# Row norms taken out of the first transposes and applied to the projections' results

## The chip, the cores and the metric

One core of a Trainium2 chip runs the whole program: one launch, all inputs in the chip's memory, float32 throughout. The metric is the device time of one execution in microseconds (us), as a median of several runs. The engines are named as in the profile: PE is TensorE (matmuls), PEld its weight loads, DVE is VectorE, ACT is ScalarE, POOL is GpSimd, SP is the engine whose queue issues most of the transfers.

## What is computed

A transformer block with a mixture of experts, followed by a convolution and recurrence block, for 256 tokens of 1024 numbers. The change touches only the beginning of the first block:

```python
hn = rmsnorm(h, attn_norm_g[layer])          # h is x, 256 x 1024
proj = hn @ w_in[layer]                      # 1024 x 2560
q, k, v, u, vg = jnp.split(proj, [512, 1024, 1536, 2048], axis=-1)
sb_out = stick_breaking_attention(q, k, v)
sg_out = chunked_spatial_gating(u, vg, ...)  # gelu(u) * mix(rmsnorm(gelu(vg)))
...
def rmsnorm(x, g):
    return x * lax.rsqrt(jnp.mean(x * x, axis=-1, keepdims=True) + EPS) * g
```

The root mean square of a row of x is one factor per token. It can be multiplied into the rows before the matmul or into the rows of the result.

## The kernel before

The kernel keeps x as the tile `h` (128 partitions, two chunks c of 128 tokens, 1024 columns). A matmul contracts over partitions, so x is transposed first: 8 column blocks kt of 128 times 2 chunks, into four PSUM tiles `pts` (two named `acc`, two named `zt`). Every weight and activation of the projections is split into a rounded part (`hi`, type fp32r) and the remainder (`lo`), and each product is three matmuls: hi·hi, lo·hi, hi·lo.

Lines 285 to 289 make the row factors: for each chunk ACT squares 1024 columns with a running sum (`ssq`), DVE turns the sum to a mean plus epsilon (`ms`, line 252), POOL raises it to -0.5 (`r1`, line 253), and DVE writes `diag`, the identity times the 128 factors. The transposes at line 300 are matmuls of `h` against `diag`, so that the rows come out transposed and scaled at once. Lines 301 to 308 split the transposed blocks: ACT writes `xT_hi` with the column gains `gcol` as its scale, DVE writes `xT_lo`. `gcol` itself is a transpose of the loaded gain rows (line 291) that DVE copies out.

The weights arrive as tiles of 1 MB in a ring of buffers, issued by SP in order; a buffer is issued again when its reader has freed it. A weight tile of the first projections is handled in four parts, called units. `Units.split` (lines 213 to 234) has ACT copy a unit to `w_hi` (line 228) and DVE, or POOL for units 30 to 39, subtract to get `w_lo` (line 229). There are three buffers of each, so the `w_hi` of unit u+3 waits until PE has finished unit u. `proj_ws(j)` (line 314) does one projection of 256 columns with the weights as the stationary side, so that the tokens lie along the free side of the result; `proj_ts(j)` (line 328) has the tokens on the partitions. Projections 0 to 3 give q and k (copied to SBUF by ACT, lines 350 and 352), 4 and 5 give v (copied by DVE, lines 446 and 450), 6 and 7 give vg, 8 and 9 give u. `gelu2` (line 428) computes gelu from a projection's PSUM tile in five steps that go back and forth between ACT and DVE; the mixing (line 488) needs the u tile `uT`, and the projection's PSUM buffer is free only after gelu2's last step (line 436).

The order of the instructions on each engine is set when the program is built, by a list scheduler with times of its own; on the chip each engine then runs its queue in that order. Before the first data has landed PE runs 12 matmuls on constants (`keep_warm`, line 186).

Of the kernel before, what the change touches and what calls it, by code (L numbers as in the profile page):

```python
# [8 lines left out]
F32 = mybir.dt.float32  # L9
# [3 lines left out]
AF = mybir.ActivationFunctionType  # L13
OP = mybir.AluOpType
# [78 lines left out]
def kernel(ctx: ExitStack, tc: tile.TileContext, a: dict, out):  # L93
    nc = tc.nc
    V, S, T, G = nc.vector, nc.scalar, nc.tensor, nc.gpsimd
# [57 lines left out]
    p1 = phase.enter_context(tc.tile_pool(name="p1", bufs=1, side="right"))  # L153
# [4 lines left out]
    p1m = work.enter_context(tc.tile_pool(name="p1m", bufs=1, side="right"))  # L158
    p1t = work.enter_context(tc.tile_pool(name="p1t", bufs=3, side="right"))
    attn = ExitStack()  # L160
    p1w = attn.enter_context(tc.tile_pool(name="p1w", bufs=2))
    psA = phase.enter_context(tc.tile_pool(name="psA", bufs=3, space=PSUM))
    psZ = phase.enter_context(tc.tile_pool(name="psZ", bufs=2, space=PSUM))
    h = keep.tile([128, 2, 1024], F32, name="h")
# [10 lines left out]
    ident = consts.tile([128, 128], F32, name="ident")  # L175
# [73 lines left out]
    def rms_scale(dst, ssq, n, mul=1.0):  # L249

        t = small.tile([128, ssq.shape[1]], F32, name="ms")
        V.tensor_scalar(t, ssq, mul / n, mul * EPS, op0=OP.mult, op1=OP.add)
        G.tensor_tensor(dst, t, mhalf[:, :ssq.shape[1]], op=OP.pow)
# [27 lines left out]
    hnl = [(p1, R)[i].tile([128, 4, 256], F32R, name=f"xT_lo{i}", tag=("a1", "r2")[i]) for i in range(2)]  # L281
    ssq = small.tile([128, 2, 2], F32, name="ssq")
    r1 = small.tile([128, 2], F32, name="r1")
    diag = p1.tile([128, 2, 128], F32, name="diag", tag="x40")
    for c in range(2):
        sq = psZ.tile([128, 1024], F32, name="zt")
        S.activation(sq, h[:, c], AF.Square, accum_out=ssq[:, c, 0:1])
        rms_scale(r1[:, c:c + 1], ssq[:, c, 0:1], 1024)
        V.tensor_scalar(diag[:, c], ident, r1[:, c:c + 1], None, op0=OP.mult)
    pg = psA.tile([128, 24], F32, name="acc")  # L290
    T.transpose(pg, rows, ident[:24, :24])
    V.tensor_copy(gcol, pg)
# [1 line left out]
    gffn = gcol[:, 16:24]  # L294
    V.tensor_mul(wr, wr, gffn[:, :, None].to_broadcast([128, 8, 40]))
    units.prep(0)
    pts = [(psA, psA, psZ, psZ)[kk].tile([128, 2, 2, 128], F32, name=("acc", "acc", "zt", "zt")[kk]) for kk in range(4)]
    for kt in range(8):
        for c in range(2):
            T.matmul(pts[kt // 2][:, kt % 2, c], h[:, c, kt * 128:(kt + 1) * 128], diag[:, c], start=True, stop=True)  # L300
    for kk in range(4):
        for kt in (2 * kk, 2 * kk + 1):
            S.activation(hnh[kt // 4][:, kt % 4], pts[kt // 2][:, kt % 2].rearrange("p c t -> p (c t)"), AF.Copy,
                         scale=gcol[:, kt:kt + 1])
        for kt in (2 * kk, 2 * kk + 1):
            V.scalar_tensor_tensor(hnl[kt // 4][:, kt % 4], pts[kt // 2][:, kt % 2].rearrange("p c t -> p (c t)"),
                                   gcol[:, kt:kt + 1], hnh[kt // 4][:, kt % 4].bitcast(F32), op0=OP.mult,
                                   op1=OP.subtract)
        if kk < 2:
            units.prep(kk + 1)  # L310

    XT = [[x[k // 4][:, k % 4] for k in range(8)] for x in (hnh, hnl)]

    def proj_ws(j):

        ps = psA.tile([128, 2, 256], F32, name="acc")
        for part in range(4):
            wh, wl = units.get(U_IN[j] + part)
            for b in range(2):
                for k in range(2):  # L320
                    kt = 2 * part + k
                    for i, (w, x) in enumerate(((wh, XT[0]), (wl, XT[0]), (wh, XT[1]))):
                        T.matmul(ps[:, b, :], w[:, k, b * 128:(b + 1) * 128], x[kt],
                                 start=kt == 0 and b == 0 and i == 0, stop=kt == 7 and i == 2, skip_group_check=True)
            units.prep(U_IN[j] + part + 3)
        return ps

    def proj_ts(j):

        ps = psA.tile([128, 2, 256], F32, name="acc")  # L330
        for part in range(4):
            wh, wl = units.get(U_IN[j] + part)
            for c in range(2):
                for k in range(2):
                    kt = 2 * part + k
                    for i, (w, x) in enumerate(((wh, XT[0]), (wl, XT[0]), (wh, XT[1]))):
                        T.matmul(ps[:, c, :], x[kt][:, c * 128:(c + 1) * 128], w[:, k, :],
                                 start=kt == 0 and c == 0 and i == 0, stop=kt == 7 and i == 2, skip_group_check=True)
            units.prep(U_IN[j] + part + 3)
        return ps  # L340

    qT = R.tile([128, 4, 256], F32, name="qT", tag="r3")
    kT = R.tile([128, 4, 256], F32, name="kT", tag="r4")
    vt = p1.tile([128, 2, 512], F32, name="vt", tag="x40")
    vg2 = p1m.tile([128, 2, 512], F32, name="vg2", tag="x41")
    mixh = [p1d.tile([128, 4, 256], F32R, name="mix_hi")]
    mixl = [p1d.tile([128, 4, 256], F32R, name="mix_lo")]

    for j in range(2):
        S.activation(qT[:, 2 * j:2 * j + 2], proj_ws(j), AF.Copy)  # L350
    for j in range(2):
        S.activation(kT[:, 2 * j:2 * j + 2], proj_ws(2 + j), AF.Copy)

# [72 lines left out]
    def gelu2(dst, ps):  # L428

        s = p1t.tile([128, 512], F32, name="gel", tag="tmp")  # L430
        f = ps.rearrange("p b t -> p (b t)")
        S.activation(s, f, AF.Square)
        V.tensor_scalar(s, s, GELU_A, 1.0, op0=OP.mult, op1=OP.add)
        V.tensor_mul(s, s, f)
        S.activation(s, s, AF.Tanh, scale=GELU_C)
        V.scalar_tensor_tensor(dst, s.rearrange("p (b t) -> p b t", b=2), 1.0, ps, op0=OP.add, op1=OP.mult)
# [6 lines left out]
                    channel_multiplier=1)  # L443

    ps = proj_ts(4)
    V.tensor_copy(vt[:, :, 0:256], ps)
    probs(0)
    scores(2)
    ps = proj_ts(5)
    V.tensor_copy(vt[:, :, 256:512], ps)  # L450
    heads_out(0)
    probs(1)
    scores(3)
    ps = proj_ts(6)
    gelu2(vg2[:, :, 0:256], ps)
    heads_out(1)
    probs(2)
    ps = proj_ts(7)
    gelu2(vg2[:, :, 256:512], ps)
    heads_out(2)  # L460
    probs(3)
# [10 lines left out]
    for c in range(2):  # L472
        sq = p1t.tile([128, 512], F32, name="gel", tag="tmp")
# [2 lines left out]
    G.tensor_tensor(rv, ssv, mhalf[:, :2], op=OP.pow)  # L476
    for c in range(2):
        V.scalar_tensor_tensor(vg2[:, c], vg2[:, c], rv[:, c:c + 1], gb512, op0=OP.mult, op1=OP.mult)
    ps = proj_ws(8)
    gelu2(uT[:, 0:2], ps)  # L480
    heads_out(3)
    attn.close()
    ring.open("c", late.enter_context(tc.tile_pool(name="ring_c", bufs=NC, reuse_waits="tile")), NC)
    ring.pump()
    ps = proj_ws(9)
    gelu2(uT[:, 2:4], ps)

    def mixing(p):
# [81 lines left out]
    for j in range(4):  # L570
        acc = psA.tile([128, 2, 256], F32, name="acc")
# [11 lines left out]
    for j in range(4):  # L583
        acc = psA.tile([128, 2, 256], F32, name="acc")
# [64 lines left out]
    pr = psM.tile([128, 2, 32], F32, name="ms")  # L649
# [135 lines left out]
    start = gather(0, 1)  # L785
# [148 lines left out]
    r1 = small.tile([128, 2], F32, name="r1")  # L934
# [27 lines left out]
    for i in range(16):  # L962
# [37 lines left out]
        for k, idx in enumerate(W_EXP[i]["w_down"]):  # L1000
            t = ring.get(idx)
            for n in range(2):
                for j in range(2):
                    m = T.matmul(dn[n][64 * j:64 * j + 64], hT[:, k, 64 * j:64 * j + 64], t[:, j, 512 * n:512 * n + 512],  # L1004
                             start=k == 0, stop=k == 3, skip_group_check=True)
# [16 lines left out]
    for n in range(2):  # L1022
        for k, idx in enumerate(W_EXP[15]["w_down"]):
# [3 lines left out]
            for j in range(2):  # L1027
                T.matmul(dn[n][64 * j:64 * j + 64], hT[:, k, 64 * j:64 * j + 64], t[:, j, 512 * n:512 * n + 512],
                         start=k == 0, stop=k == 3, skip_group_check=True)
# [21 lines left out]
    diag = q0.tile([128, 2, 128], F32, name="diag2")  # L1051
# [506 lines left out]
```

## Time and profile before

| | |
|---|---|
| median of 3 runs | 1062.04 us |
| lowest and highest run | 1059.91 and 1063.41 us |
| the profiled execution's own time | 1064.05 us |
| span of its records | 1062.3 us |
| PE busy in the span | 1030.8 us (97%) |
| DVE, ACT, POOL busy | 531.5, 368.4, 226.6 us |
| moved by DMA | 300.23 MB |

The profiled execution is 2.0 us above the median of the runs, and 1.7 us of its time lies outside the span of the records. The stages follow each other: transposes and first projections to about 88 us, output projection and routing to 123 us, the experts to 582 us, the second block to the end.

A row of the timeline gives start, duration, engine, line, operation, written tile and read tiles, shapes and count, and in brackets the idle time of the engine before it with what ended it. Several equal instructions in a row are merged into one line of the timeline, whose duration goes from the first start to the last end.

### The profile page before, as it was taken

The numbers are of one execution on the slowest core, as the hardware profiler recorded it, in microseconds if no ns is written. First come the engines' busy times: TensorE is split into PE (matmuls) and PEld (weight loads), VectorE is DVE, ScalarE is ACT, GpSimd is POOL, SyncE is SP. The second block draws the span as 40 slices with busy tenths as digits, with TensorE's granted clock in tenths as the row PEclk, the third lists the DMA queues.
The fourth block names the chain that finished last, engine by engine and source line by source line (L and its number), as shares of the span: only waits on it lengthen the run. The fifth ranks groups of instructions, "written<-read, shape, count | busy, mean of one in ns | idle before, by whom it ended". The sixth has DMA issues, their size and how long they took to land.

```text
span 1062.3 us, 16320 instructions
## 1 busy us (share of the span) xinstructions
PE 1030.8 (97%) x6660; PEld 742.5 (70%) x6660; DVE 531.5 (50%) x1014; ACT 368.4 (35%) x595; POOL 226.6 (21%) x135
## 2 busy tenths in 40 slices
PE   8999999999999999999999999996999999999997
PEld 7998644444444444444443999876999999998996
DVE  4758432222222222222223588888947676556555
ACT  5565311000000000000001654857546446444443
POOL 0262000000000000000000887654876900000000
PEclk9999999999999999999999999998999999999999
DMA  9987899899999999999999855422553666655531
GB/s 317 303 349 275 313 366 411 332 409 409 409 409 409 409 409 409 409 408 409 409 408 387 259 192 178 141 80 80 199 164 118 202 211 198 199 189 177 192 116 40
DMA packets 139131, 300.23 MB, mean 283 GB/s; under 512 B 14341, under 2 KB 79341, under 8 KB 139053
## 3 DMA queue, kind: packets, MB, share of 16 engines
q1 hardware_dynamic: 138541, 297.84, 76.3%
q8 instruction: 53, 0.87, 0.3%
q10 hardware_dynamic: 432, 1.05, 0.3%
q0 software_dynamic: 80, 0.26, 0.1%
q14 instruction: 25, 0.20, 0.1%
HBM read 298.08 MB, written 1.05 MB: 282 GB/s over the span
## 4 chain that ended last, share of the span: by engine, by line
PE 77%; DMA 2%; ACT 1%; DVE 1%; issue 1%; POOL 0%; POOLq 0%; ACTq 0%
PE acc L1120 26%; PE gate L834 9%; PE up L834 9%; PE dn L1004 9%; PE acc L1456 8%; PE ms L680 5%; PE acc L1386 3%; PE ms L733 3%; PE acc L1429 2%; DMA ring_a<-in_w_down_dram 2%; PE acc L1239 1%; PE acc L1244 1%; PE ms L720 1%; ACT w_hi L228 0%; PE ms L701 0%
## 5 line engine op out<-in xcount | busy, mean ns | idle before, releaser
L229 POOL TENSOR_TENSOR w_lo<-ring_a,w_hi 128x1024 fp32r<-128x1024 f32 (+1 forms) x77 | 184.0, 2404 | 516.1 <-PE ms L733 457.5
L228 ACT ACTIVATE w_hi<-ring_a 128x1024 fp32r<-128x1024 f32 (+1 forms) x169 | 169.0, 1003 | 131.9 <-PE acc L1120 34.2
L229 DVE TENSOR_TENSOR w_lo<-ring_a,w_hi 128x1024 fp32r<-128x1024 f32 (+1 forms) x92 | 101.8, 1109 | 69.9 <-ACT w_hi L228 69.8
L1120 PE MATMUL acc<-n_hi,w_hi 128*128 128x256 f32 x448 | 117.5, 289 | 13.4 <-DVE vb L1273 12.1
L1120 PE MATMUL acc<-n_hi,w_lo 128*128 128x256 f32 x448 | 116.3, 287 | 0.0
L1176 DVE SCALAR_TENSOR_TENSOR acc<-ub,pcol,acc 128x256 f32<-128x256 f32 x232 | 105.7, 485 | 7.2 <-ACT acc L1171 1.6
L739 DVE TENSOR_TENSOR h<-h,ms 128x512 f32<-128x512 f32 x60 | 38.6, 684 | 125.6 <-PE ms L733 125.6
L1120 PEld LDWEIGHTS acc<-n_hi,w_hi 128*128 128x128 f32 x448 | 86.2, 193 | 16.9 <-ACT acc L1290 8.8
L726 ACT ACTIVATE y<-dn 128x512 fp32r<-128x512 f32 x30 | 17.9, 598 | 213.8 <-PE ms L733 99.8
L1120 PEld LDWEIGHTS acc<-n_hi,w_lo 128*128 128x128 f32 x448 | 86.3, 193 | 0.5 <-issue 0.4
L1120 PE MATMUL acc<-n_lo,w_hi 128*128 128x256 f32 x448 | 82.3, 286 | 0.0
L727 DVE TENSOR_TENSOR y<-dn,y 128x512 fp32r<-128x512 f32 x30 | 20.6, 688 | 110.9 <-ACT y L726 110.9
L680 PEld LDWEIGHTS ms<-onehot,x_moe 128*128 128x128 f32 x512 | 59.8, 192 | 14.8 <-issue 13.0
L1120 PEld LDWEIGHTS acc<-n_lo,w_hi 128*128 128x128 f32 x448 | 66.7, 193 | 0.0
L680 PE MATMUL ms<-onehot,x_moe 128*128 128x128 f32 x512 | 64.4, 279 | 0.8 <-DVE onehot L670 0.8
L1120 PE MATMUL acc<-x2h,w_hi 128*128 128x256 f32 x256 | 64.5, 280 | 0.0
L1120 PE MATMUL acc<-x2h,w_lo 128*128 128x256 f32 x256 | 64.5, 280 | 0.0
L1004 PE MATMUL dn<-ring_b,hs_hT 128*64 128x512 f32 x240 | 57.0, 597 | 0.0
L1456 PE MATMUL acc<-w_hi,fh 128*128 128x512 f32 x128 | 50.0, 391 | 0.0
L1456 PE MATMUL acc<-w_lo,fh 128*128 128x512 f32 x128 | 49.9, 390 | 0.0
L1456 PE MATMUL acc<-w_hi,fl 128*128 128x512 f32 x128 | 49.5, 390 | 0.0
L1120 PEld LDWEIGHTS acc<-x2h,w_hi 128*128 128x128 f32 x256 | 48.3, 189 | 0.6
(373 smaller groups left out, 2016.0 us busy)
## 6 DMA issues: line engine op xcount, KB each, us to landing
ring_a<-in_w_in_dram SPq DMA_DIRECT2D x32, 1024.0 KB, 5.1
ring_a<-in_w_dram SPq DMA_DIRECT2D x32, 1024.0 KB, 4.7
ring_b<-in_w_down_dram SPq DMA_DIRECT2D x30, 1024.0 KB, 18.5
ring_b<-in_w_gate_dram SPq DMA_DIRECT2D x26, 1024.0 KB, 18.4
ring_b<-in_w_up_dram SPq DMA_DIRECT2D x25, 1024.0 KB, 18.5
ring_a<-in_w_gate_dram SPq DMA_DIRECT2D x18, 1024.0 KB, 14.8
ring_a<-in_w_up_dram SPq DMA_DIRECT2D x15, 1024.0 KB, 12.2
ring_a<-in_w_down_dram SPq DMA_DIRECT2D x14, 1024.0 KB, 18.5
```

The lines of the kernel that those rows point to most:

```text
L228: S.activation(hi[:, s], src[:, s], AF.Copy)
L229: steps.append(lambda s=s: E.tensor_sub(lo[:, s], src[:, s], hi[:, s].bitcast(F32)))
L680: T.matmul(p[:, k], xp[c][:, 128 * (k0 + k):128 * (k0 + k + 1)], g[:, c], start=c == 0, stop=c == 1)
L733: T.matmul(p, gt[:m, c], y[:m, k], start=k == 0, stop=k == 1)
L739: V.tensor_add(h[:, c, s], h[:, c, s], to_token(gt, c, m, y))
L834: m = T.matmul(ps[64 * j:64 * j + 64, :], x[:, 2 * q + k, 64 * j:64 * j + 64], t[:, j, 512 * k:512 * k + 512], start=q == 0 and k == 0, st ...
L1004: m = T.matmul(dn[n][64 * j:64 * j + 64], hT[:, k, 64 * j:64 * j + 64], t[:, j, 512 * n:512 * n + 512], start=k == 0, stop=k == 3, skip_gr ...
L1120: T.matmul(ps[:, b, :], w[:, k, b * 128:(b + 1) * 128], xx[4 * half + k], start=half == 0 and b == 0 and k == 0 and w is wh and not low, s ...
L1176: V.scalar_tensor_tensor(ca[:, j] if k == 30 else s, ub[:, j, k:k + 256], conv_a_w[:, 8 * k + j:8 * k + j + 1], s, op0=OP.mult, op1=OP.add)
L1386: T.matmul(pb[b // 2][:, b % 2, :], w[:, kk, b * 128:(b + 1) * 128], xx[:, kt], start=kt == 0 and b % 2 == 0 and q == 0, stop=kt == 11 and ...
L1429: T.matmul(p[:, c], xx[:, kt, 128 * c:128 * c + 128], w[:, k, :], start=half == 0 and k == 0 and c == 0 and q == 0, stop=half == 1 and k = ...
L1456: T.matmul(out_ps[c][n], f[:, half, 128 * c:128 * c + 128], w[:, 0, 512 * n:512 * n + 512], start=j == 0 and half == 0 and q == 0, stop=j ...
```

## The change

The transposes no longer carry the row factors. They become plain transposes of `h` against the identity, issued chunk by chunk, and `diag` is gone. The split of the transposed blocks is as before, on unscaled values. The squares are four of 512 columns with their result in SBUF, the two chunks' factors are computed in one go, and `r1` is used later: for q, k and u (tokens along the free side) the factors are spread over all partitions by two matmuls of a broadcast column against the identity and copied by ACT to `rb`, and DVE multiplies each projection's PSUM tile by it; for v and vg (tokens on partitions) DVE multiplies by the column `r1`, chunk by chunk.

```diff
-    diag = p1.tile([128, 2, 128], F32, name="diag", tag="x40")
-    for c in range(2):
-        sq = psZ.tile([128, 1024], F32, name="zt")
-        S.activation(sq, h[:, c], AF.Square, accum_out=ssq[:, c, 0:1])
-        rms_scale(r1[:, c:c + 1], ssq[:, c, 0:1], 1024)
-        V.tensor_scalar(diag[:, c], ident, r1[:, c:c + 1], None, op0=OP.mult)
...
-    for kt in range(8):
-        for c in range(2):
-            T.matmul(pts[kt // 2][:, kt % 2, c], h[:, c, kt * 128:(kt + 1) * 128], diag[:, c], start=True, stop=True)
+    for c in range(2):
+        for kt in range(8):
+            T.transpose(pts[kt // 2][:, kt % 2, c], h[:, c, kt * 128:(kt + 1) * 128], ident)
...
+    for c in range(2):
+        for n in range(2):
+            sq = p1w.tile([128, 512], F32, name="sq0", tag="tanh")
+            S.activation(sq, h[:, c, 512 * n:512 * n + 512], AF.Square, accum_out=ssq[:, c, n:n + 1])
+    V.tensor_add(ssq[:, :, 0], ssq[:, :, 0], ssq[:, :, 1])
+    rms_scale(r1, ssq[:, :, 0], 1024)
+    rb = p1m.tile([128, 256], F32, name="rb")
...
+    def scaled_ws(dst, j):
+
+        ps = proj_ws(j)
+        if j == 0:
+            pr = psA.tile([128, 256], F32, name="acc")
+            for c in range(2):
+                T.matmul(pr[:, 128 * c:128 * c + 128], r1[:, c:c + 1].to_broadcast([128, 128]), ident, start=True,
+                         stop=True)
+            S.activation(rb, pr, AF.Copy)
+        V.tensor_mul(ps if dst is None else dst, ps, rb[:, None, :].to_broadcast([128, 2, 256]))
+        return ps
+
     for j in range(2):
-        S.activation(qT[:, 2 * j:2 * j + 2], proj_ws(j), AF.Copy)
+        scaled_ws(qT[:, 2 * j:2 * j + 2], j)
     for j in range(2):
-        S.activation(kT[:, 2 * j:2 * j + 2], proj_ws(2 + j), AF.Copy)
+        scaled_ws(kT[:, 2 * j:2 * j + 2], 2 + j)
...
     ps = proj_ts(4)
-    V.tensor_copy(vt[:, :, 0:256], ps)
+    for c in range(2):
+        V.tensor_scalar(vt[:, c, 0:256], ps[:, c], r1[:, c:c + 1], None, op0=OP.mult)
...
     ps = proj_ts(6)
+    for c in range(2):
+        V.tensor_scalar(ps[:, c], ps[:, c], r1[:, c:c + 1], None, op0=OP.mult)
     gelu2(vg2[:, :, 0:256], ps)
...
-    ps = proj_ws(8)
+    ps = scaled_ws(None, 8)
     gelu2(uT[:, 0:2], ps)
...
-    ps = proj_ws(9)
+    ps = scaled_ws(None, 9)
     gelu2(uT[:, 2:4], ps)
```

What is left out of the diff treats projections 5 and 7 as 4 and 6. Line numbers after the change differ: line 300 (transposes) becomes 295, 303 (`xT_hi`) 298, 306 (`xT_lo`) 301, 323 (matmuls of `proj_ws`) 326, 436 (last step of gelu2) 451, 499 (`sg`) 520. The scaling by `rb` is line 361, the two matmuls that make it line 358.

How the order of the instructions moves, at three places. First ACT at the very start; `xT_hi_182` holds the column blocks kt 0 to 3, `xT_hi_183` the blocks 4 to 7. Before:

```order
L287 ACTIVATE zt,ssq<-h 128x1024 x2
L228 ACTIVATE w_hi<-ring_a 128x512 x3
L303 ACTIVATE xT_hi_182<-acc,gcol 128x256 x4
L303 ACTIVATE xT_hi_183<-zt,gcol 128x256 x4
L228 ACTIVATE w_hi<-ring_a 128x512 x4
L350 ACTIVATE qT<-acc 128x512
```

After, from the last of the four squares on:

```order
L310 ACTIVATE sq_247,ssq<-h 128x512
L228 ACTIVATE w_hi<-ring_a 128x512 x2
L298 ACTIVATE xT_hi_183<-zt,gcol 128x256 x3
L298 ACTIVATE xT_hi_182<-acc,gcol 128x256 x2
L298 ACTIVATE xT_hi_183<-zt,gcol 128x256
L298 ACTIVATE xT_hi_182<-acc,gcol 128x256 x2
L228 ACTIVATE w_hi<-ring_a 128x512 x2
L360 ACTIVATE rb<-acc 128x256
```

The squares still stand first, two `w_hi` instead of three stand ahead of the split of x, and block kt 0 is the fourth block of the split instead of the first.

Second, PE from its last `keep_warm` matmul on. Before:

```order
L291 MATMUL acc<-ident,rows 128x24
L300 MATMUL acc<-diag,h 128x128 x2
L300 MATMUL zt<-diag,h 128x128 x2
L300 MATMUL acc<-diag,h 128x128 x6
L300 MATMUL zt<-diag,h 128x128 x6
L323 MATMUL acc<-xT_hi_182,w_hi 128x256
L323 MATMUL acc<-xT_hi_182,w_lo 128x256
L323 MATMUL acc<-xT_lo_184,w_hi 128x256
```

After:

```order
L295 MATMUL zt<-ident,h 128x128 x8
L285 MATMUL acc<-ident,rows 128x24
L295 MATMUL acc<-ident,h 128x128 x8
L326 MATMUL acc<-xT_hi_182,w_hi 128x256
L326 MATMUL acc<-xT_hi_182,w_lo 128x256
L326 MATMUL acc<-xT_lo_184,w_hi 128x256
```

The transposes now wait for x alone and stand ahead of the gain rows. Third, DVE around the gelu of projections 8 and 9; `uT` is gelu's last step, `sg` the product of mixing and `uT`. Before:

```order
L436 SCALAR_TENSOR_TENSOR uT<-gel,acc 128x512
L229 TENSOR_TENSOR w_lo<-ring_b,w_hi 128x512 x2
L252 TENSOR_SCALAR ms<-sums 128x2
L499 TENSOR_TENSOR sg<-acc,uT 128x256
L229 TENSOR_TENSOR w_lo<-ring_b,w_hi 128x512
L433 TENSOR_SCALAR gel<-gel 128x512
L499 TENSOR_TENSOR sg<-acc,uT 128x256
L434 TENSOR_TENSOR gel<-gel,acc 128x512
L426 SCALAR_TENSOR_TENSOR mix_lo_1155<-sg,gcol,mix_hi_1154 128x256 x2
L436 SCALAR_TENSOR_TENSOR uT<-gel,acc 128x512
```

After:

```order
L229 TENSOR_TENSOR w_lo<-ring_b,w_hi 128x512
L451 SCALAR_TENSOR_TENSOR uT<-gel,acc 128x512
L361 TENSOR_TENSOR acc<-acc,rb 128x512
L229 TENSOR_TENSOR w_lo<-ring_b,w_hi 128x512
L520 TENSOR_TENSOR sg<-acc,uT 128x256 x2
L448 TENSOR_SCALAR gel<-gel 128x512
L449 TENSOR_TENSOR gel<-gel,acc 128x512
L441 SCALAR_TENSOR_TENSOR mix_lo_1167<-sg,gcol,mix_hi_1166 128x256 x2
L451 SCALAR_TENSOR_TENSOR uT<-gel,acc 128x512
```

The multiplication of projection 9 by `rb` stands between the first `uT` and the steps that lead to the second.

## Rows read from the trace of the kernel before

**Rows 1.** The page: busy time, and the chain that ended last by engine.
```profile
PE 1030.8 (97%) x6660; PEld 742.5 (70%) x6660; DVE 531.5 (50%) x1014; ACT 368.4 (35%) x595; POOL 226.6 (21%) x135
...
PE 77%; DMA 2%; ACT 1%; DVE 1%; issue 1%; POOL 0%; POOLq 0%; ACTq 0%
```

**Rows 2.** Timeline of PE, 0 to 14 us: start, duration, instruction, idle before.
```profile
1.24 4.49 PE L190 MATMUL acc<-ones_b 128*128 128x512 bf16 x12 [1.24 <-DVE ones_b L182]
6.94 0.21 PE L291 MATMUL acc<-ident,rows 24*128 24x24 f32 x1 [1.21 <-DMA rows<-in_ffn_norm_g_dram]
...
10.09 1.50 PE L300 MATMUL zt<-diag,h 128*128 128x128 f32 x12
11.35 0.36 PE L323 MATMUL acc<-xT_hi,w_hi 128*128 128x256 f32 x1
11.55 0.28 PE L323 MATMUL acc<-xT_hi,w_lo 128*128 128x256 f32 x1
11.67 0.28 PE L323 MATMUL acc<-xT_lo,w_hi 128*128 128x256 f32 x1
```

**Rows 3.** Timeline of ACT, 0 to 16 us.
```profile
5.92 1.03 ACT L287 ACTIVATE zt<-h 128x1024 f32<-128x1024 f32 x1 [0.23 <-DMA h<-in_x_dram]
...
8.22 1.15 ACT L228 ACTIVATE w_hi<-ring_a 128x512 fp32r<-128x512 f32 x2 [1.15 <-DMA ring_a<-in_w_in_dram]
...
10.17 1.56 ACT L303 ACTIVATE xT_hi<-acc,gcol 128x256 fp32r<-128x256 f32 x4
11.60 1.59 ACT L303 ACTIVATE xT_hi<-zt,gcol 128x256 fp32r<-128x256 f32 x4
...
14.54 0.63 ACT L228 ACTIVATE w_hi<-ring_a 128x512 fp32r<-128x512 f32 x1 [0.81 <-PE acc L323]
```

**Rows 4.** Timeline of DVE, 4 to 16 us.
```profile
8.88 2.11 DVE L229 TENSOR_TENSOR w_lo<-ring_a,w_hi 128x512 fp32r<-128x512 f32 x3 [0.29 <-ACT w_hi L228]
11.03 1.66 DVE L306 SCALAR_TENSOR_TENSOR xT_lo<-acc,gcol,xT_hi 128x256 fp32r<-128x256 f32 x4
```

**Rows 5.** Groups by line, 0 to 120 us: busy us, mean ns, idle before.
```profile
L434 DVE TENSOR_TENSOR gel<-gel,acc 128x512 f32<-128x512 f32 x4 | 2.7, 685 | 0.3
...
L555 PE MATMUL zt<-ident,h 128*128 128x128 f32 x16 | 2.6, 276 | 0.0
...
L499 DVE TENSOR_TENSOR sg<-acc,uT 128x256 f32<-128x256 f32 x4 | 1.6, 421 | 0.3 <-issue 0.2
L474 ACT ACTIVATE gel<-vg 128x512 f32<-128x512 f32 x2 | 1.2, 615 | 0.0
```

**Rows 6.** Line 1362, the same spreading matmul later on: ns, first and last start.
```profile
L1362 PE MATMUL acc<-ident,rl x4: 270/274/275, 805.1 to 805.4; 128*128 128x128 f32 x4
```

**Rows 7.** Timeline of PE, 183 to 190 us.
```profile
187.42 0.73 PE L733 MATMUL ms<-y,onehotT 128*128 128x512 f32 x2 [1.06 <-DVE y L727]
188.78 1.71 PE L834 MATMUL gate<-ring_a,xg 128*64 128x512 f32 x4 [0.62 <-PEq L845]
```

**Rows 8.** Windows: length, busy by engine, PE's granted clock, DMA share, GB/s.
```profile
188.00:189.00 1.00, 0.38 (x3) 0.23 (x4) 1.00 (x2) 0.00 (x0) 0.00 (x0) 1.00 1.01 406
...
190.00:191.00 1.00, 1.00 (x4) 0.30 (x2) 0.13 (x1) 0.00 (x0) 0.00 (x0) 0.50 1.01 401
```

**Rows 9.** The chain that ended last, 188 to 240 us: start, length, what.
```profile
188.78 8.78 PE gate L834 x32
...
216.21 6.87 PE gate L834 x32
```

**Rows 10.** Timeline of DVE, 37 to 40 us.
```profile
39.52 0.43 DVE L372 TENSOR_SCALAR om<-tanh 128x512 f32<-128x512 f32 x1 [0.53 <-POOL tanh L367]
```

**Rows 11.** Timeline of DVE, 82 to 90 us.
```profile
87.49 0.68 DVE L436 SCALAR_TENSOR_TENSOR uT<-gel,acc 128x512 f32<-128x512 f32 x1
```

**Rows 12.** Timeline of PE, 87 to 88.5 us.
```profile
88.23 0.39 PE L538 MATMUL acc<-w_hi,mix_hi 128*128 128x256 f32 x1 [0.34 <-DVE uT L436]
```

**Rows 13.** Timeline of PE, 571 to 576 us, the end of the experts.
```profile
575.36 1.08 PE L1028 MATMUL gate<-ring_a,hs_hT 128*64 128x512 f32 x4 [0.29 <-DMA ring_a<-in_w_down_dram]
```

More of the change, by code (lines that the diff above doesn't have):

```diff
@@ L449 @@
     ps = proj_ts(5)
-    V.tensor_copy(vt[:, :, 256:512], ps)
+    for c in range(2):
+        V.tensor_scalar(vt[:, c, 256:512], ps[:, c], r1[:, c:c + 1], None, op0=OP.mult)
     heads_out(0)
@@ L454 @@
     ps = proj_ts(6)
+    for c in range(2):
+        V.tensor_scalar(ps[:, c], ps[:, c], r1[:, c:c + 1], None, op0=OP.mult)
     gelu2(vg2[:, :, 0:256], ps)
@@ L458 @@
     ps = proj_ts(7)
+    for c in range(2):
+        V.tensor_scalar(ps[:, c], ps[:, c], r1[:, c:c + 1], None, op0=OP.mult)
     gelu2(vg2[:, :, 256:512], ps)
```

## Prediction

> **What bounds the kernel now.** I read the page first: PE is busy for 97% of the span and holds 77% of the chain that ended last [rows 1]. So the question for any change at the beginning is only this: by how much does it move the point from which PE runs without a gap, and does it open a new gap later?
>
> Then the timeline of PE over the first 14 us [rows 2]. The reader should see three things: the warm-up matmuls from 1.24 to 5.73 us, a hole until 6.94, and the first matmul of projection 0 at 11.35, with the transposes ending just before it. From there PE goes on at 0.12 us per matmul (11.55 to 11.67), 12 matmuls or 1.44 us per unit. So before the change the transposes are the last thing that projection 0 waits for, and they wait for the row factors.
>
> Third, the timelines of ACT and DVE over the same time [rows 3, 4], because ACT's order decides the start after the change. ACT gets the second half of x at 5.92 us, waits for the first weights until 8.22, rounds two units, and splits the transposed blocks at one per 0.36 us ((11.60 - 10.17) / 4).
>
> Does an earlier or later PE at 11 us reach the end? The last gap of the experts ends on a weight transfer, but by only 0.29 us [rows 13]. The ring's buffers are issued again as PE frees them, so the stream of transfers moves with PE. I count a shift at the beginning in full at the end.
>
> **What goes away.** 16 scaled transposes: 6 of them are 12 passes in 1.50 us, so one is two passes, 0.24 us [rows 2]. A plain transpose is one pass: 16 transposes are 16 records [rows 5]. PE saves 16 passes of 0.11, some 1.8 us, and no longer waits for the factors. The new queue of PE is 8 transposes from 5.73 to 6.65, the gain rows at 6.94 (they had landed by then), 8 transposes until about 8.0. So PE is done with them 3.3 us earlier than before. On ACT four squares of 512 columns cost 0.615 each [rows 5] in place of two of 1024 at 1.03 [rows 3]: from 5.92 the second chunk is done by about 7.2, still ahead of 8.22. Nothing there reaches the path.
>
> **What projection 0 then waits for.** ACT. Its queue has the squares, two `w_hi`, and then the blocks with kt 0 in fourth place. The weights land at 8.22 as before. Two `w_hi` take 1.15 - 0.63 = 0.52 us from start to start, so the split starts at 9.27, kt 0 starts three blocks later at 10.35, and ends 0.48 later (1.56 - 3 x 0.36) [rows 3]: 10.83. Against 11.35 that is **0.5 us earlier**, not 3.3. The second operand `xT_lo` comes from DVE, third in its row there: `w_lo` twice until 10.1, then one block per 0.39 us [rows 4], kt 0 done at about 11.3; PE's third matmul waits for it by about 0.2 us. The bounds: if the weights land when they did, nothing can be earlier than 10.4 (kt 0 without the wait behind its last neighbour) or later than 11.4 (every block at the 0.39 us of DVE). That is -0.9 to 0.
>
> **What is added to PE.** Two float32 matmuls of 128 x 128 to spread the factors, in the middle of projection 0's second unit: four passes. The same instruction later takes 0.3 us from first to last start and 0.27 for the last one [rows 6]. I take **+0.5** (0.45 to 0.6). The factors are ready long before: squares done at 7.2, mean and POOL's power about 1 us more, against 12.8 for the matmuls. If that cover were gone, each microsecond would count.
>
> **The clock of PE.** Between 8.0 and 10.83 PE has nothing to do: 2.8 us in one piece. Before the change its longest hole there was 1.21 us [rows 2], and the clock stayed. Where it did not stay is at 188 us: after holes of 1.06 and 0.62 us [rows 7] the granted clock went from 1.00 to 0.50, that is from 2.4 to 1.2 GHz, while PE had already begun work again [rows 8]. The gate matmuls of that pair took 8.78 us and those of the next pair 6.87 [rows 9]: **1.9 us** lost. A hole of 2.8 us is longer than both together, so I expect the same fall just before or at the start of projection 0, at the same price, +1.9; the bounds are 0 and +2.0. Half-speed matmuls also hide the 0.2 us wait for `xT_lo`, so I don't add it.
>
> [...]
>
> **What is added to DVE.** Six multiplications of 128 x 512 by `rb` at 0.69 and eight of 128 x 256 by `r1` at 0.42 [rows 5], less two copies at about 0.69: 4.1 + 3.4 - 1.4 = 6.1 us over some 70. ACT loses four copies. Each unit has slack: `w_hi` is made three units ahead (it waits 0.81 us for PE [rows 3]) and needs 0.63 + 0.69 of 2.88 us, so 1.5 us may be lost to other work on DVE. For q and k the multiplication falls in DVE's waits for `w_hi`; the last one, behind the scans of the first attention pair, uses the 0.53 us that DVE waits for POOL there [rows 10]. For v two times 0.42 stand for 0.69. I cost these at nothing; uncovered they would be some 1 us.
>
> The place without cover is the gelu of projection 9. Its PSUM buffer is wanted by the first output matmul, which waited 0.34 us for DVE's last step at 87.49 to 88.17 [rows 11, 12]. Now a multiplication of 0.69 stands at the head of that chain (projection 9 ends at about 84.0), then ACT's square and the rest. Following the new queue: multiplication 84.05 to 84.7, `w_lo` 85.4, two `sg` 86.1, gelu's steps until 87.1, two `mix_lo` 87.9, last step 88.55. So **+0.4** against 88.17; bounds -0.3 (another buffer comes free first, and the old wait goes too) and +1.4 (both multiplications of u uncovered).
>
> **Sum.** -0.5 + 0.5 + 1.9 + 0.4 = **+2.3 us**. Against the profiled execution's own 1064.05 that is 1066.35; but that execution is 2.0 above the median, about the price of the one fall of the clock that it shows. I add the sum to the median: 1062.04 + 2.3 = **1064.3 us**.
>
> **Rivals.**
> - The clock holds. For it: no fall at 5.73 to 6.94, nor elsewhere in the head. Against it: the hole is more than twice as long. Then the wait for `xT_lo` counts: -0.5 + 0.2 + 0.5 + 0.4 = +0.6, 1062.6 us.
> - DVE becomes the late engine between 75 and 88 us, and it ends slower: the two multiplications of u are each serial with ACT's square behind them, and if DVE has no gap left for either, 2 x 0.69 and the waits that they lengthen (0.8) come instead of 0.4. It decides as soon as the last gelu step ends later than 88.9. +2.3 - 0.4 + 2.2 = +4.1, 1066.1 us. For it: DVE's last step already ends a wait of PE there [rows 12]; against: the first multiplication falls into a time when DVE waits for ACT.
> - The change brings what it could: the split starts right at 8.2 (weights that land 1 us earlier than here would do it), kt 0 ends at 8.22 + 3 x 0.36 + 0.48 = 9.8, the hole is short and the clock holds: -1.55 + 0.2 + 0.5 + 0.4 = -0.45, 1061.6 us; if the shift also spares the fall at 188 us, 1.9 less, 1059.7. Against it stands ACT's queue: the `w_hi` are ahead.
>
> **How the numbers follow.** [...] About 0.3% (3.2 us) is what a measurement of this kernel can tell from no change: faster is below 1058.9, slower above 1065.2. The forecast is 0.9 below that edge, and the runs lie up to 2.1 below and 1.4 above their median, so a quarter of its 0.58 and three quarters of DVE's 0.14 fall beyond: slower 0.25, faster 0.04, same 0.71. The range takes in the clock's rival, the bounds of the mixing's term and DVE's rival, and leaves out half of the last case: 1061.0 to 1066.8.
>
> **What would show it.** In the timeline of PE: transposes done by 8.0, first projection matmul at about 10.8, and then matmuls 0.24 us apart instead of 0.12 for some 3 us, with a granted clock of 0.50 in the windows. ACT's `xT_hi` from 9.3 on. The wait before the first output matmul 0.7 to 0.8 instead of 0.34. I am wrong if the first matmul comes before 10, if its neighbours stay 0.12 apart, or if PE shows waits for DVE between 35 and 75 us.

## The result, and the profile after

The changed kernel takes 1069.76 us as a median of 12 runs (1066.25 to 1071.22), against 1062.47 us for 12 runs of the kernel before beside it. The medians lie 7.3 us apart. The ratio on record is 1.0056, with an interval of 1.0047 to 1.0065, which is 6.0 us (5.0 to 6.9). The kernel before had medians from 1062.47 to 1063.73 us in the four sets of runs of this case, so the text compares by ratios. By either measure the change is slower, above the range of the prediction. The profiled execution took 1070.28 us, its span is 1068.6 us, and PE is busy for 1034.5 us of it, still 97%.

Where the 6 us come from is found by following the same points through both traces. The `w_hi` of unit 4 starts at 14.54 us before and at 15.87 after: +1.33. The first attention output matmul of head pair 2 stands at 74.24 and 75.92: +1.68. The first output projection matmul stands at 88.23 [rows 12] and 93.91: +5.68. The first gate matmul of the expert pair at 188.78 [rows 7, 9] now comes at 195.60: +6.82. Later the shift is 6.20 (a chain of matmuls that starts at 895.60 starts at 901.80), and the span ends 6.3 us later. So in these two executions the head costs 1.3 us. The 60 us behind it cost 0.35, where PE waits 0.35 us for `w_lo` from POOL at 72.85. The 20 us around the mixing cost **5.1**: 4.0 until the first output matmul, and 1.1 because the output matmuls begin at half clock (0.21 us apart until 96.42).

First the head, in PE's timeline of the changed kernel, and at the end ACT's `w_hi` of unit 4:

```profile
5.41 1.03 PE L295 MATMUL zt<-ident,h 128*128 128x128 f32 x8
...
6.69 1.09 PE L295 MATMUL acc<-ident,h 128*128 128x128 f32 x8
10.07 0.39 PE L326 MATMUL acc<-xT_hi,w_hi 128*128 128x256 f32 x1 [2.29 <-ACT xT_hi L298]
...
10.96 0.39 PE L326 MATMUL acc<-xT_lo,w_hi 128*128 128x256 f32 x1 [0.38 <-DVE xT_lo L301]
...
11.74 0.41 PE L326 MATMUL acc<-xT_hi,w_hi 128*128 128x256 f32 x1
11.96 0.41 PE L326 MATMUL acc<-xT_hi,w_lo 128*128 128x256 f32 x1
...
13.45 1.05 PE L358 MATMUL acc<-ident,r 128*128 128x128 f32 x4
...
15.87 0.63 ACT L228 ACTIVATE w_hi<-ring_a 128x512 fp32r<-128x512 f32 x1 [0.94 <-PE acc L326]
```

The transposes are done at 7.78, PE has nothing to do for 2.29 us, and projection 0 begins 1.28 us earlier than before [rows 2]. Then its matmuls stand 0.21 us apart and not 0.12. The windows of the same kernel show the granted clock (length, PE busy and its instructions, the clock as a share of the full one, DMA share, GB/s), at the head and again around the mixing:

```profile
10.00:12.00 2.00, 1.55 (x8) 0.81 1.08 358
12.00:14.00 2.00, 2.00 (x11) 0.50 1.11 350
14.00:16.00 2.00, 2.00 (x16) 0.83 1.10 348
...
82.00:84.00 2.00, 1.07 (x11) 1.00 0.33 41
84.00:86.00 2.00, 1.59 (x15) 1.00 0.83 317
86.00:88.00 2.00, 2.00 (x12) 0.59 1.01 414
88.00:90.00 2.00, 2.00 (x14) 0.50 1.02 420
...
94.00:96.00 2.00, 2.00 (x10) 0.50 0.06 16
96.00:98.00 2.00, 2.00 (x16) 0.85 0.45 40
```

The second fall is the larger one: some 10 us at a granted clock of 0.50. PE's rows there, with the wait ahead of the fall:

```profile
82.57 0.50 PE L423 MATMUL sums<-ones,sqs 128*128 128x1 f32 x4
84.41 0.65 PE L512 MATMUL acc<-brow,ident 8*64 8x256 f32 x4 [1.33 <-issue]
84.99 0.66 PE L517 MATMUL acc<-WT,vg 128*64 128x128 f32 x8
...
87.61 1.12 PE L512 MATMUL acc<-brow,ident 8*64 8x256 f32 x4
...
93.91 0.58 PE L559 MATMUL acc<-w_hi,mix_hi 128*128 128x256 f32 x1
```

The first mixing matmul (line 512) waits 1.33 us. The profile names "issue", which is not a releaser. But the matmul begins 0.10 us after an instruction of DVE that frees one of the three PSUM buffers named `acc`: `mix_lo` of the last head pair, which ends at 84.31. DVE's timeline in the changed kernel:

```profile
78.64 0.69 DVE L361 TENSOR_TENSOR acc<-acc,rb 128x512 f32<-128x512 f32 x1
79.56 2.94 DVE L499 SCALAR_TENSOR_TENSOR vg<-vg,rv,gb 128x512 f32<-128x512 f32 x2 [0.23 <-POOL rv L497]
82.42 1.49 DVE L448 TENSOR_SCALAR gel<-gel 128x512 f32<-128x512 f32 x1
83.84 0.47 DVE L441 SCALAR_TENSOR_TENSOR mix_lo<-acc,gcol,mix_hi 128x256 fp32r<-128x256 f32 x1
```

And the same place in the kernel before, DVE's rows and then PE's, which show no wait ahead of the mixing:

```profile
79.46 0.69 DVE L434 TENSOR_TENSOR gel<-gel,acc 128x512 f32<-128x512 f32 x1
80.07 0.48 DVE L426 SCALAR_TENSOR_TENSOR mix_lo<-acc,gcol,mix_hi 128x256 fp32r<-128x256 f32 x1
80.46 1.96 DVE L478 SCALAR_TENSOR_TENSOR vg<-vg,rv,gb 128x512 f32<-128x512 f32 x2
```

```profile
80.98 0.65 PE L491 MATMUL acc<-brow,ident 8*64 8x256 f32 x4
...
84.32 0.65 PE L491 MATMUL acc<-brow,ident 8*64 8x256 f32 x4
84.90 0.66 PE L496 MATMUL acc<-WT,vg 128*64 128x128 f32 x8
...
87.23 0.66 PE L496 MATMUL acc<-WT,vg 128*64 128x128 f32 x8
```

`mix_lo` comes 3.77 us later. 1.68 of that is the shift that PE has too (DVE's `ssv` stands at 76.18 and 77.86), 0.69 the new multiplication (line 361). The other 1.4 go with the order: before, `mix_lo` stood ahead of the two normalizations of `vg`; after, it stands behind them, and they are slow there (2.94 us against 1.96). Of the 5.1 us, 1.75 are lost when the first mixing matmul begins (84.41 against 80.98, less the 1.68), and the other 3.4 behind it, where the clock falls to half.

### The profile page after: what moved, and what is told of

Its sections match the earlier page's. It is cut to its first block, busy times and chain, and to the rows that moved or that the text cites. A ratio compares the mean times of both kernels' runs of the same rounds, so it can differ in the third digit from the quotient of the medians.

```text
span 1068.6 us, 16300 instructions
## 1 busy us (share of the span) xinstructions
PE 1034.5 (97%) x6648; PEld 744.4 (70%) x6648; DVE 538.8 (50%) x1024; ACT 367.8 (34%) x596; POOL 226.1 (21%) x134
## 3 DMA queue, kind: packets, MB, share of 16 engines
q10 hardware_dynamic: 432, 1.05, 0.2%
HBM read 298.08 MB, written 1.05 MB: 280 GB/s over the span
## 4 chain that ended last, share of the span: by engine, by line
PE 76%; DMA 2%; ACT 1%; DVE 1%; issue 0%; POOL 0%; POOLq 0%; ACTq 0%
PE acc L1141 25%; PE gate L855 9%; PE up L855 9%; PE dn L1025 9%; PE acc L1477 8%; PE ms L701 5%; PE acc L1407 3%; PE ms L754 3%; PE acc L1450 2%; DMA ring_a<-in_w_down_dram 2%; PE acc L1260 1%; PE acc L1265 1%; PE ms L741 1%; ACT w_hi L228 0%; PE ms L722 0%
```

## The experiments

A first theory, A, held that the multiplications added on DVE make it late at the mixing. Its rival B was at first that the shifted start of the projections does it. After the first four runs B became more exact: the list scheduler turned round the order of `mix_lo` and the two normalizations, and the order opens the hole. The table has all runs; the last column is the start of the same gate matmul in the profiled execution (188.78 before, 195.60 changed). Each run has one trace, and executions of one kernel differ by some us: the changed kernel's go from 1066.25 to 1071.22.

| run | what it is | median us | ratio to before, interval | gate, us |
|---|---|---|---|---|
| e1 | changed, u not multiplied | 1066.10 | 1.0023 (1.0012 to 1.0035) | 196.75 |
| e2 | changed head alone, no multiplication | 1067.53 | 1.0032 (1.0021 to 1.0044) | 193.02 |
| e3 | before, with the multiplications | 1069.52 | 1.0048 (1.0032 to 1.0063) | 195.45 |
| e4 | changed, mixing in other buffers | 1063.67 | 0.9999 (0.9989 to 1.0009) | 189.75 |
| e5 | changed, hole of the head filled | 1069.13 | 1.0057 (1.0040 to 1.0074) | 194.13 |
| e6 | changed, `mix_lo` first again | 1065.88 | 1.0019 (1.0009 to 1.0029) | 191.72 |
| e7 | before, with the order of after | 1067.62 | 1.0045 (1.0030 to 1.0059) | 191.95 |
| e8 | changed, hole at the mixing filled | 1068.54 | 1.0055 (1.0038 to 1.0072) | 190.56 |
| e9 | changed, e4 and a head by hand | 1061.22 | 0.9979 (0.9968 to 0.9989) | 188.07 |
| e10 | before, mixing in other buffers | 1063.56 | 1.0002 (0.9993 to 1.0010) | 189.32 |

**e1, u without its factors.**

```diff
-    ps = scaled_ws(None, 8)
+    ps = proj_ws(8)
...
-    ps = scaled_ws(None, 9)
+    ps = proj_ws(9)
```

> The changed kernel without the two multiplications of u (projections 8 and 9) by the tokens' factors; its output is therefore another one. Theory A: the 6 us of the change are two holes of PE, each followed by a fall of the granted clock: about 1.3 us at the head (a hole of 2.3 us before projection 0) and about 5 us around the mixing (a hole of 1.3 us at 83.1 us while the first mixing matmul waits for a PSUM buffer that DVE's mix_lo at 84.31 frees late, then half clock from 86.3 to 96.5). If u's first multiplication, at 78.64 to 79.33 and 0.69 long, is what makes DVE late, the hole shrinks below 0.4 us, the clock stays at 1.00 there, and the time is about 1064 to 1065. If the scaling of vg or the order on DVE (two normalizations of vg ahead of gelu's step and mix_lo) is what counts, mix_lo stays later than 83 us, the hole stays above 0.7 us and the time stays at 1067 or more.

Measured: 1066.10 us, but from 1064.54 to 1071.74, and the profiled execution is the slowest. In it the hole is not gone; it is 1.54 us long, and `mix_lo` still starts at 83.45, behind normalizations of 2.92 us:

```profile
84.03 1.02 PE L512 MATMUL acc<-brow,ident 8*64 8x256 f32 x4 [1.54 <-issue]
```

So u's multiplications are not needed for the hole, against A's first branch. But by the ratios the run gives back 0.33 of the 0.56%. The mean granted clock is 0.981 in the profiled execution and 0.986 to 0.991 in the nine others, so this trace does not stand for them: they ran less at half clock, and why leaving out u's multiplications did that no trace shows.

**e2, the head alone, and e3, the multiplications alone.**

For e2, against the changed kernel (v and vg likewise):

```diff
-        scaled_ws(qT[:, 2 * j:2 * j + 2], j)
+        S.activation(qT[:, 2 * j:2 * j + 2], proj_ws(j), AF.Copy)
```

> Only the head of the change: plain transposes, squares and factors as in the changed kernel, but nothing is multiplied by the factors and they are not spread; q, k and v are copied as before. Its output lacks the row norms. Theory A: the head's hole and fall of the clock are there (granted clock 0.50 from 11 to 14 us), worth 1.3 us less the 0.5 to 1 of the two spreading matmuls, and the mixing is as in the kernel before: about 1062.5 to 1063.5. Rival B: the late start of projection 0 by itself, not the multiplications, brings DVE and the PSUM buffers out of step at the mixing; then the second fall of the clock is here too and the time is 1067 to 1069.

For e3, against the kernel before (the other projections as in the change):

```diff
-        S.activation(qT[:, 2 * j:2 * j + 2], proj_ws(j), AF.Copy)
+        scaled_ws(qT[:, 2 * j:2 * j + 2], j)
```

> The kernel before with its scaled transposes, and the multiplications of the results by the factors, with the two spreading matmuls, added on top, so that the factors count twice and the output is another one. Theory A: no fall of the clock in the head (first projection matmul at 11.3 us, clock 1.00), but the hole before the first mixing matmul and the half clock for some 10 us after it: about 1067 to 1068. Rival B: no hole at the mixing and about 1062.5 to 1063.5.

Measured: 1067.53 and 1069.52. Each half of the change by itself loses more than half of the whole loss by its ratio (0.32, with 0.21 to 0.44, and 0.48 of 0.56%); the halves don't add up. In e2, without one multiplication, PE has the same hole, and here the profile names its releaser:

```profile
82.03 0.50 PE L423 MATMUL sums<-ones,sqs 128*128 128x1 f32 x4
83.77 0.78 PE L506 MATMUL acc<-brow,ident 8*64 8x256 f32 x4 [1.24 <-DVE mix_lo L441]
84.48 1.12 PE L511 MATMUL acc<-WT,vg 128*64 128x128 f32 x8
```

In e3, with a head as before (clock 1.00 until 84 us), the hole is 1.84 us. Neither theory as first put explains both. What the changed kernel, e1, e2 and e3 share is DVE's order: the normalizations stand ahead of `mix_lo` in all four, and in the kernel before behind it. This is where the new theory B comes from.

**e4, other PSUM buffers for the mixing.**

```diff
-        m = psA.tile([128, 2, 128], F32, name="acc")
+        m = psZ.tile([128, 2, 128], F32, name="zt")
```

> The whole changed kernel, but the PSUM tile of the mixing comes from the two buffers named zt, which are free by then, and not from the three named acc. Theory A: the first mixing matmul no longer waits for mix_lo, PE has no hole above 0.4 us between 80 and 88 us, the granted clock stays 1.00 there, and the time is about 1064 to 1065.5. Rival C: the clock falls because the narrow mixing matmuls stand in a row without projection matmuls between them, hole or not; then the half clock is still there from 86 us on and the time stays at 1068 or more. If DVE's lateness only moves on to the next reader (sg and uT), a wait of PE for uT or for an acc buffer of about 1 us appears between 86 and 93 us.

Measured: 1063.67 us, the time of the kernel before. `mix_lo` is as late as it was (83.32 us, still behind the normalizations), but the mixing does not wait for it, and the narrow mixing matmuls run at 0.65 us a group:

```profile
71.90 1.07 PE L512 MATMUL zt<-brow,ident 8*64 8x256 f32 x6
79.83 0.66 PE L517 MATMUL zt<-WT,vg 128*64 128x128 f32 x8
82.04 0.66 PE L517 MATMUL zt<-WT,vg 128*64 128x128 f32 x8
```

```profile
82.00:84.00 2.00, 2.00 (x20) 1.00 0.90 215
84.00:86.00 2.00, 2.00 (x20) 1.00 1.02 420
86.00:88.00 2.00, 2.00 (x18) 1.00 1.03 422
```

PE is full and the clock stays at 1.00 from 80 to 88 us. But the scheduler also rearranged PE: the first narrow matmuls (line 512) now come over 12 us earlier, and no row of narrow matmuls stands between 80 and 88 us. So e4 changes more than the wait, and it does not test rival C, which needs the narrow matmuls in a row. The kernel before does: there they stand in a row from 83.95 to 87.89, and the clock is 1.00 in the windows from 82 to 90 us:

```profile
84.00:86.00 2.00, 2.00 (x21) 1.00 1.07 395
86.00:88.00 2.00, 1.89 (x22) 1.00 0.96 375
```

Rival C (the narrow matmuls alone) falls by that.

**e10, the same buffers in the kernel before.**

> The kernel before with one thing changed: the mixing's PSUM tile comes from the zt buffers. Tells what that choice is worth without the change. In the kernel before PE waits only 0.34 us there, and the clock stays at 1.00, so at most 0.4 us are to be had: 1062.5 to 1063.5. If it gains more than 1 us, part of what the same edit gave back to the changed kernel is its own and not the removal of the hole.

Measured: 1063.56, no difference (0.9993 to 1.0010), although PE's order moves here as in e4. So the buffers with their new order are worth nothing where there is no hole, which speaks for the hole as what e4 took away.

**e6, the order turned back in the changed kernel.** The normalizations are issued after `mix_lo`; all multiplications stay.

```diff
-    for c in range(2):
-        V.scalar_tensor_tensor(vg2[:, c], vg2[:, c], rv[:, c:c + 1], gb512, op0=OP.mult, op1=OP.mult)
...
-    heads_out(3)
+    last = heads_out(3)
+    with tc.issue_after(last.ins):
+        for c in range(2):
+            V.scalar_tensor_tensor(vg2[:, c], vg2[:, c], rv[:, c:c + 1], gb512, op0=OP.mult, op1=OP.mult)
```

> The whole changed kernel, with one thing moved in DVE's row: the two normalizations of vg (2.9 us beside POOL's subtractions) stand behind the mix_lo that frees the PSUM buffer for the mixing, as in the kernel before, and not ahead of it. New theory B: in the changed kernel and in the three runs that lost time so far these two stood ahead of mix_lo; in the kernel before they stood behind it. The scheduler turned this order round because the edit shifted its own times, and that order, not the multiplications themselves, opens the hole of PE. Then here: no hole over 0.5 us between 80 and 88 us, clock 1.00 there, and 1064 to 1065.5. If the multiplications of vg and u on DVE are the cause (theory A), mix_lo still comes too late, the hole stays over 0.8 us and the time at 1067 or more.

Measured: 1065.88 us; by the ratios (0.19% for 0.56%) 3.9 us less than the changed kernel (some 2.5 to 5.3, an estimate from the two intervals). DVE's and PE's rows:

```profile
82.52 0.48 DVE L441 SCALAR_TENSOR_TENSOR mix_lo<-acc,gcol,mix_hi 128x256 fp32r<-128x256 f32 x1
82.91 2.03 DVE L503 SCALAR_TENSOR_TENSOR vg<-vg,rv,gb 128x512 f32<-128x512 f32 x2
```

```profile
83.46 0.65 PE L513 MATMUL acc<-brow,ident 8*64 8x256 f32 x4
84.03 0.60 PE L423 MATMUL sums<-ones,sqs 128*128 128x1 f32 x4
...
91.17 0.39 PE L560 MATMUL acc<-w_hi,mix_hi 128*128 128x256 f32 x1 [0.38 <-DVE uT L451]
```

There is no hole ahead of the mixing, the clock stays at 1.00 from 80 to 100 us, and the wait before the output projection is 0.38. What is left is 0.19%. This execution has the hole (2.63 us) and the fall at the head, and 2.12 of its 2.94 us at the gate are there already at the `w_hi` of unit 4 (16.66). But it is 1.85 us above e6's median, and e4, whose head is the same, loses nothing, so where the 0.19% of the median lie is not shown.

**e7, that order in the kernel before,** and nothing else of the change; PE's first mixing matmuls, with those on `vg` right behind, are put where the changed kernel has them. (In e6 PE's order there went back too, so the share of DVE's order alone is not measured.)

```diff
-        V.scalar_tensor_tensor(ml, o, g, mh.bitcast(F32), op0=OP.mult, op1=OP.subtract)
+        with tc.issue_after(norm.ins) if (part, p) == (0, 3) else ExitStack():
+            V.scalar_tensor_tensor(ml, o, g, mh.bitcast(F32), op0=OP.mult, op1=OP.subtract)
```

> The kernel before, with nothing of the change but the order at the mixing: DVE does the two normalizations of vg ahead of mix_lo, and PE does the first mixing matmuls, with those on vg right behind, after 37 of projection 9's 48 matmuls, as in the changed kernel. Theory B: mix_lo ends at about 83 us and not at 80.55, PE has a hole of 1 to 2 us before the first mixing matmul, the clock falls behind it, and the time is 1066 to 1068. Theory A (the added multiplications are needed for the hole): at most 0.5 us more than before, 1063 to 1064.

Measured: 1067.62 us, 0.45% slower than the kernel before. The hole and the fall are there without any multiplication and without the new head; later PE waits 1.06 us for `uT`, where it waits 0.34 in the kernel before:

```profile
82.64 0.65 PE L496 MATMUL acc<-brow,ident 8*64 8x256 f32 x4 [1.52 <-issue]
83.22 0.77 PE L501 MATMUL acc<-WT,vg 128*64 128x128 f32 x8
```

```profile
82.00:84.00 2.00, 1.36 (x13) 0.91 0.41 55
84.00:86.00 2.00, 2.00 (x9) 0.50 0.91 348
86.00:88.00 2.00, 2.00 (x17) 0.74 1.03 420
```

B stands from both sides: the order of before takes the time away in e6, and the order of after brings it in e7. Theory A, that the multiplications are needed for the hole, falls. That they make it dearer is not excluded (e1).

**e5 and e8, holes filled with matmuls on constants.** e5 puts ten of them ahead of projection 0, e8 six ahead of the first mixing matmul.

```diff
+        for _ in range(10 if j == 0 else 0):
+            T.matmul(ps.rearrange("p b t -> p (b t)"), ones_b, ones_b[:, 0:1].to_broadcast([128, 512]), start=True, stop=True)
```

> The changed kernel with ten matmuls on constants (128 x 512, bf16), put in PE's row between the transposes and projection 0, into the PSUM tile that projection 0 then overwrites. They fill the hole of 2.3 us. If the hole is what lets the clock fall at the head, the granted clock stays 1.00 until 16 us and the matmuls of the first units stand 0.12 us apart; the fourth unit's w_hi comes at about 14.6 in place of 15.87, and the time falls by 1.0 to 1.3 us to about 1068.5; the hole and the half clock at the mixing stay. If the fall of the head has another cause, the clock falls as before and the time stays at 1069.8.

```diff
+    with tc.issue_after(nine[36]):
+        for _ in range(6):
+            T.matmul(warm, ones_b, ones_b[:, 0:1].to_broadcast([128, 512]), start=True, stop=True)
```

> The whole changed kernel, with six matmuls on constants (128 x 512, bf16) put in PE's row between the 37th matmul of projection 9 and the first mixing matmul, which still waits for mix_lo. They fill the hole of 1.33 us with work that nobody needs. If the hole only costs by the fall of the clock behind it, the granted clock stays 1.00 from 84 to 97 us and the time falls by 3.5 to 4 us to about 1066; if the row of narrow mixing matmuls or the short waits behind are what lets the clock fall, the half clock stays and the time is 1069 to 1070.

Measured: in e5 the clock stays at 1.00 until 84 us and `w_hi` of unit 4 comes at 14.50. That fits the hole being what lets the clock fall at the head; so do the other traces with this head, where the clock fell behind holes of 2.07 (e1), 2.12 (e2), 2.29 (changed) and 2.63 us (e6), and did not behind 1.95 (e4) and 1.49 us (e8). But e5's median, 1069.13, is within the scatter of the changed kernel. PE reaches the mixing 1.97 us earlier (80.60 against 82.57), DVE's `mix_lo` 1.47 (82.37 against 83.84), so the hole there is 1.84 us where it was 1.33: 0.50 of what was won at the head is lost again in front of DVE. The other 1.47 are still there at the gate matmul of this execution (194.13 against 195.60). Four runs from 1068.62 to 1070.88 can't show whether the median gains that, so e5 answers for the clock, in one execution, and not for the time.

In e8's profiled execution the clock stays at 1.00 through the head and the mixing and it took 1065.31 us; the three others took 1067.84 to 1070.34. The mean granted clock was 0.991 in the first and 0.990, 0.986 and 0.986 in the others (0.983 to 0.989 in the changed kernel), and no trace tells where it fell. e8 is inconclusive.

**e9, a version that gains.** e4's buffers, and a head in an order written by hand:

```diff
+    head.enter_context(tc.manual_schedule(engines={T.engine, V.engine, S.engine}))
...
+    for c in range(2):
+        for kt in range(4):
+            T.transpose(pts[kt // 2][:, kt % 2, c], h[:, c, kt * 128:(kt + 1) * 128], ident)
+    T.transpose(pg, rows, ident[:24, :24])
...
+    for kk in range(4):
+        for kt in (2 * kk, 2 * kk + 1):
+            S.activation(hnh[kt // 4][:, kt % 4], pts[kt // 2][:, kt % 2].rearrange("p c t -> p (c t)"), AF.Copy,
+                         scale=gcol[:, kt:kt + 1])
+        if kk < 3:
+            steps = units.split()
+        for kt in (2 * kk, 2 * kk + 1):
+            V.scalar_tensor_tensor(hnl[kt // 4][:, kt % 4], pts[kt // 2][:, kt % 2].rearrange("p c t -> p (c t)"),
+                                   gcol[:, kt:kt + 1], hnh[kt // 4][:, kt % 4].bitcast(F32), op0=OP.mult,
+                                   op1=OP.subtract)
+        if kk < 3:
+            for step in steps:
+                step()
```

> The whole changed kernel with the mixing in the zt buffers (as in the earlier run of that form) and the head in an order written out by hand: PE transposes the column blocks 0 to 3 first, DVE copies the gains before it handles the squares' sums, and ACT and DVE alternate two blocks of x with one unit of weights, beginning with blocks 0 and 1. If projection 0 was late in the changed kernel because ACT did two units of weights and blocks 4 to 6 ahead of block 0, the first projection matmul now comes at 8.5 to 9.0 us and not at 10.07, the hole before it is below 1.2 us and the clock stays at 1.00; unit 4's w_hi comes at 12 to 13 us and not at 14.5 (before) or 15.9 (changed). That is 1.5 to 2.5 us to the better of the kernel before at the head, and nothing lost at the mixing: 1060.5 to 1062. If the second tile half of weights or DVE (one unit and two blocks cost it 1.4 us, as much as PE takes for a unit) holds projection 0's later units, the gain at unit 4 is below 0.7 us and the time equals the kernel before, 1063.

Measured: 1061.22 us, ratio 0.9979 (0.9968 to 0.9989): 2.2 us faster than the kernel before by the ratio. In its profiled execution the transposes began at 6.34 us (5.41 in the changed kernel's) and the matmul on the gain rows behind the first eight came at 7.75 (6.55). The first projection matmul stands at 9.65 and not at 8.5 to 9.0, and `w_hi` of unit 4 at 13.71 and not at 12 to 13, 0.83 us ahead of the kernel before where 1.5 to 2.5 were expected. Still the hole is short and the clock holds:

```profile
7.92 1.09 PE L299 MATMUL zt<-ident,h 128*128 128x128 f32 x8
9.65 0.39 PE L332 MATMUL acc<-xT_hi,w_hi 128*128 128x256 f32 x1 [0.64 <-ACT w_hi L228]
```

## Why the prediction was wrong, point by point

- **PE saves 16 passes and is done early.** Right: done at 7.78, 8.0 was said.
- **ACT sets the start of projection 0.** Right as a mechanism. It was put at 2.61 us behind the first weights (10.83 against 8.22); measured 2.66, 2.65 and 2.66 behind them in the changed kernel, e8 and e6, with the first `w_hi` at 7.41, 7.11 and 8.18. The clock time 10.07 lies ahead of the bound of 10.4, because the bound took the weights' landing as fixed; the first `w_hi` moves by 1.1 us between these executions.
- **Two matmuls at line 358, +0.5.** Right: 0.60 at full clock in e4, 1.05 at half.
- **The clock falls in the head, +1.9.** It fell, and cost less. Counted from the first `w_hi`, the `w_hi` of unit 4 comes 8.46 us later in the changed kernel, and 6.97, 6.95 and 6.95 in e4, e8 and e5, where the clock stayed: 1.5 us. In e4 and e8 the hole was 1.95 and 1.49 us, so the fall is not certain in every execution. The chances were 0.58 for the forecast with its fall, 0.20 for a clock that holds, 0.14 for "DVE late" and 0.08 for a change that pays; some 0.05 of the 0.58 was for a fall that is certain, which no run shows. In three runs it did not come: from the end of the last constant matmul to the first projection matmul PE had only transposes and the hole, from 6.28 to 10.29 in e4, 6.21 to 9.76 in e8 and 6.54 to 9.65 in e9, and the clock stayed at 1.00. What the transposes and what the plain hole do to the clock can't be told apart by these runs. The prediction's 2.4 and 1.2 GHz are in the traces the granted shares 1.00 and 0.50: at 1.00 the 32 gate matmuls of 512 columns took 6.87 us [rows 9], 2.4 columns per ns, and at 0.50 the changed kernel's matmuls of 256 columns stood 0.21 us apart, 1.2 columns per ns.
- **Multiplications of q, k and v at nothing.** Right within 0.5 us, as far as one execution shows: in e5, with a head that keeps its clock, the attention output of pair 2 stands at 73.95, before at 74.24.
- **The mixing, +0.4, bounds -0.3 to +1.4.** This is the step that failed; 5.1 us was measured in the profiled executions. The step followed DVE's rows around projection 9's gelu, where the multiplication adds 0.7 us. It did not follow the rows a little ahead, where `mix_lo`, the instruction that frees the buffer for the first mixing matmul, had gone behind two normalizations. Its bounds priced instructions, not a fall of the clock behind a hole, although the head's term had done just that with the fall at 188 us [rows 7 to 9]. The wait before the first output matmul, forecast at 0.7 to 0.8 us, is gone: DVE's last step ends at 92.70, and PE at half clock comes there only at 93.91.
- **The rival "DVE late"** pointed to the right place and side, but by another mechanism (uncovered multiplications, +4.1 us). e2 and e7 have none of them and lose 0.32 and 0.45%.
- **The sum.** +2.3 left out the turned order at the mixing. e6, where `mix_lo` stands first again, measures 0.19%, 2.0 us (1.0 to 3.1); the order is 3.9 us between e6 and the changed kernel. That e6 comes near +2.3 is partly luck. Its trace is of a slower execution: there the head's terms (-0.5 + 0.5 + 1.9 = +1.9) measure 2.12 at unit 4, and the mixing's +0.4 is 0.04 (a wait of 0.38 for 0.34). In the changed kernel the same head terms measure 1.33, with a first `w_hi` that starts 0.81 us earlier than before.

## What to carry to other kernels

Where a list scheduler sets the order, an edit at the start can turn round two instructions 70 us later; compare the whole order of both kernels, and look first for instructions that free a buffer for the engine that bounds the kernel. Price a new hole of that engine with the fall of the clock that may follow it, not with its own length: of the 5.1 us around the mixing, 3.4 came behind the hole of 1.33 us. In e4 one line, a buffer that needn't be waited for, gave back the whole loss although `mix_lo` stayed as late as it was; it also moved PE's order, so compare that again after such an edit.

## What the runs showed of the hardware

In these traces the length of a hole did not tell the price of the fall behind it. Around the mixing, holes of 1.24 (e2), 1.52 (e7), 1.33 (changed) and 1.54 us (e1) were followed by half clock for some 3.4, 3.4, 10.2 and 13.6 us (from the windows of 2 us: a window at 0.59 counts 1.64 of its 2 us as half). At the head, a hole of 1.95 us (e4) was followed by none, and one of 2.07 (e1) by some 3.4 us of half clock.

DVE and POOL slowed each other here where both worked on SBUF. Two normalizations took 2.03 us in e6, where POOL works beside them for the first 0.82 us, and 2.94 in the changed kernel, where it works all through them. Line 448, 0.42 us in projection 9's gelu with POOL idle, took 1.49 beside the second of these two subtractions of POOL, and that subtraction took 1.71 where the first took 1.29:

```profile
79.50 1.29 POOL L229 TENSOR_TENSOR w_lo<-ring_b,w_hi 128x512 fp32r<-128x512 f32 x1
...
81.91 1.71 POOL L229 TENSOR_TENSOR w_lo<-ring_b,w_hi 128x512 fp32r<-128x512 f32 x1
```

The gelu step (line 448) that began at 82.42 ended at 83.91, 0.29 us after POOL's subtraction had ended at 83.62. Why the two slow each other these runs do not show.
